# First projection chunk of a decoder trunk: quarters of x and single weight pieces, one token tile at a time

## The chip, the cores and the metric

One core of a Trainium2 chip runs the whole program: one launch, no other core involved. The metric is the device time of one execution in microseconds (us). Shown are the median of three runs and, beside it, one further execution taken by the hardware profiler, from which all rows come.

## The reference, cut to what matters

Two layers of a decoder trunk over 256 tokens of width 1024. Each layer normalizes x, projects it to retention heads, sparse-attention heads and a gated MLP, mixes them, projects back and adds; then it normalizes again and applies a SwiGLU FFN of width 2816.

```python
for l in range(DEPTH):                      # 2
    h = rms_norm(x, attn_norm[l])           # x: (1, 256, 1024)
    proj = h @ w_in[l]                      # 1024 x 3218
    r_q, r_k, r_v, r_g, n_q, n_kv, n_g, gm_z = jnp.split(proj, split_points, axis=-1)
...
    x = x + (mix @ w_out[l]).astype(x.dtype)
    h = rms_norm(x, ffn_norm[l])
    gate, up = jnp.split(h @ w_gate_up[l], 2, axis=-1)
    x = x + ((jax.nn.silu(gate) * up) @ w_down[l]).astype(x.dtype)
```

The change touches only the start of layer 0: the loads of x and of the first weights, the first normalization, and the first chunk of the product with w_in.

## The kernel before, in words

**Products.** All large products are made in three parts. An operand is split into a "hi" part (rounded to fp32r) and a "lo" part (the rest), and hi·hi, lo·hi and hi·lo are added up in a PSUM bank ("acc"). The tokens are two tiles t of 128; the contraction over 1024 is eight steps k of 128. w_in is cut by columns into seven chunks, computed in the order of ORDER; the first, "nk", has 512 columns: keys and values of the sparse attention. So it takes 8 k x 2 tiles x 3 = 48 products of 512 columns.

**Weights.** They stream from DRAM in pieces of one or two k, laid out in the order of use (PIECES; KSPLIT, line 50, gives the k in each piece of a chunk). stream_load (line 484) takes a staging buffer ("wst", at first also four pieces of the tile "PT") and issues the transfer on SP's queue. stream_hi (499) casts it on ScalarE into "whi"; stream_lo (507) subtracts on VectorE into "wlo" and gives the staging buffer back. Six buffers each of whi and wlo.

**x.** It is loaded in four quarters (t, c): tile t and half c of the 1024 columns, that is k 0 to 3 or 4 to 7. norm_first(c) (line 748) waits for both tiles' quarter c, transposes two k of both tiles into one "sm" bank with TensorE, scales by the norm's gain on ScalarE into the hi half of the tile "hcat" (hh) and makes the lo half (hl) on VectorE, 256 columns at a time. The row factor 1/rms (rstd) comes from squares made afterwards and is applied to the products' results.

**Order.** The instructions of each engine stand in the order in which a planner (class Desk) issues them. Every piece of work is a thread that yields operations, waits for events or asks for a buffer. The planner keeps a clock for each engine with costs of its own (_cost_DMA and the like; TensorE's count double until COLD, line 269; the DMA's clock begins at 2000 ns, line 274), always serves the engine that can start first, and there the request of the lowest priority number (rank, line 371). Its costs decide the order, not what is waited for: on the chip each instruction waits for its true inputs, behind what stands before it on its engine.

**The start.** load_start (594) issues the parameters on ScalarE's queue, and on SP's the identity and then the steps of START (line 157): two quarters of x, two weight pieces, two quarters, two pieces; after them the constants. warm_up (579) fills TensorE with products of a zeroed buffer ("w2k") into an sm bank while nothing else is ready, 256 columns wide until the planner's COLD and 128 after, until `started` is set, which project does at its end. In the profile one such filler is two records. setup_bias (659) puts one small product ("rbw") between, for a table of attention biases that goes to DRAM (scr) and comes back as B on SP's queue.

**The first chunk.** project (1442) with apart == "first" goes through k one after another in `both`: hi·hi for both tiles, then lo·hi for both, then hi·lo for both:

```python
            for ev in x_wait[0] + [self.split_hi[i]] if apart else x_wait[1] + [self.ready[i]]:
                yield ev
...
        if apart == "first":
            for k, (i, a) in enumerate(ks):
                yield from both(k, i, a)
```

Of the kernel before, what the change touches and what calls it, by code (L numbers as in the profile page):

```python
# [9 lines left out]
F32 = mybir.dt.float32  # L10
F32R = mybir.dt.float32r
I32 = mybir.dt.int32
AF = mybir.ActivationFunctionType
ALU = mybir.AluOpType
# [32 lines left out]
    "rg": [(_RG, 384)],  # L47
}
ORDER = ["nk", "nq", "gm", "nv", "rq", "rk", "rg"]
KSPLIT = {ORDER[0]: (1, 1, 2, 2, 2), "nv": (3, 3, 2)}  # L50


def _width(name):
# [100 lines left out]


FIRST, SLOT, GRAIN = 16512, 32, 512
START = [(0, 0), (1, 0), "w", "w", (0, 1), (1, 1), "w", "w"]

NR, NREP = 33, 3

# [18 lines left out]
def _free(ap):  # L179
    n = 1  # L180
    for s in ap.shape[1:]:
        n *= s
    return n
# [6 lines left out]
class Engine:  # L190


    def __init__(self, name, eng):
        self.name, self.eng = name, eng

    def __getattr__(self, method):
        fn = getattr(self.eng, method)
# [32 lines left out]
        return 0.833 * _free(a[0]) + (51 if _psum(a[1]) else 93) + 93 * ptr, table  # L230

    def _cost_DMA(self, method, a, k):
        return 4 * _free(a[0]) * a[0].shape[0] / 360.0 + 60, None

    def _cost_SWDMA(self, method, a, k):
        return 1060, None
# [29 lines left out]
class Desk:  # L266
    LAT = {"PE": 170, "DVE": 150, "ACT": 190, "POOL": 200, "DMA": 2000, "SWDMA": 4500}
    TABLE = 1300
    COLD = 5500.0

    def __init__(self, preload):
        self.preload = preload
        self.free = {e: 0.0 for e in self.LAT}
        self.free["DMA"] = 2000.0
        self.pending = {e: [] for e in self.LAT}
        self.table = None
        self.cur = None
        self.live = 0
        self.after = 0
        self.banks = {}  # L280
        self.given = 100
# [116 lines left out]
class Trunk:  # L398
    def __init__(self, ctx, tc, x, wts, cst, oh, relb, par, w1, w2, wsT, out):
        self.ctx, self.tc, self.nc = ctx, tc, tc.nc  # L400
        nc = self.nc
        self.d = dict(x=x, wts=wts, cst=cst, oh=oh, relb=relb, par=par, w1=w1, w2=w2, wsT=wsT, out=out)
        self.PE, self.V = Engine("PE", nc.tensor), Engine("DVE", nc.vector)
        self.A, self.G = Engine("ACT", nc.scalar), Engine("POOL", nc.gpsimd)
        self.SP, self.GQ = Engine("DMA", nc.sync), Engine("SWDMA", nc.gpsimd)

        def preload(table):
            if table == "lnexp":
                nc.scalar.preload_act_table_set("natural_log_exp_and_others")

        self.desk = Desk(preload)
        self.keep = ctx.enter_context(tc.tile_pool(name="keep", bufs=1))
        psum = ctx.enter_context(tc.tile_pool(name="psum", bufs=1, space=bass.MemoryType.PSUM))
        bank = lambda n: psum.tile([128, 512], F32, tag=n, name=n)
        self.acc = Pool([bank(f"acc{i}") for i in range(4)])
        self.sm = Pool([bank(f"sm{i}") for i in range(4)])
        self.norms = 0
        self.kept = 0

        self.pad(FIRST)  # L420
        self.wst = Pool([self.fixed(f"wst{i}", [128, 1024]) for i in range(3)])
        self.whi = Pool([self.fixed(f"whi{i}", [128, 1024], F32R) for i in range(6)])
        self.wlo = Pool([self.fixed(f"wlo{i}", [128, 1024], F32R) for i in range(6)])
        self.w2k = Pool([self.fixed(f"w2k{i}", [128, 512]) for i in range(6)])
        self.w1k = Pool([self.fixed(f"w1k{i}", [128, 256]) for i in range(4)])
        self.x = [self.fixed(f"x{t}", [128, D]) for t in range(2)]
        self.hx = self.fixed("hcat", [128, KD, 2, T], F32R)
        self.hh, self.hl = self.hx[:, :, 0, :], self.hx[:, :, 1, :]
        self.tinies = {}
        n = L * len(PIECES)  # L430
        self.loaded = [Event() for _ in range(n)]
        self.split_hi = [Event() for _ in range(n)]
        self.ready = [Event() for _ in range(n)]
        self.hi, self.lo, self.st = {}, {}, {}
        self.used = 0
        self.started = False
        self.extra = []
# [141 lines left out]
    def warm_up(self):  # L579

        w = yield Need(self.w2k)
        yield self.V.memset(w, 0.0)
        yield self.A.activation(w[:, 511:512], w[:, 510:511], AF.Gelu_apprx_tanh)
        ps = yield Need(self.sm)
        while not self.started:
            n = 256 if self.desk.free["PE"] < Desk.COLD else 128
            yield self.PE.matmul(
                ps[:, :n], w[:, :128], w[:, :n], start=True, stop=True, lat=False,
                prio=lambda: -5 if self.started else 2000,
            )  # L590
        self.desk.give(self.sm, ps)
        self.desk.give(self.w2k, w)

    def load_start(self):
# [150 lines left out]
        self.desk.give(self.w2k, junk)  # L745
        self.desk.fire(ss[c])

    def norm_first(self, c):

        gain = lambda k: self.par[:, P_G1 + k : P_G1 + k + 1]  # L750
        lat = self.desk.LAT
        for t in range(2):
            yield self.ev_x[t][c]
        for ks in ((4 * c, 4 * c + 1), (4 * c + 2, 4 * c + 3)):
            ps = yield Need(self.sm)
            p4 = ps.rearrange("p (k t n) -> p k t n", k=2, t=2)
            yield [
                self.transpose(p4[:, j, t], self.x[t][:, k * 128 : k * 128 + 128])
                for j, k in enumerate(ks)
                for t in range(2)  # L760
            ]
            yield self.ev_par[0]
            split = [Event(), Event()]
            flat = ps.rearrange("p (k n) -> p k n", k=2)

            def low(ps=ps, ks=ks, split=split, flat=flat):
                for j, k in enumerate(ks):
                    yield split[j]
                    yield self.V.scalar_tensor_tensor(
                        self.hl[:, k, :], flat[:, j], gain(k), self.hh[:, k, :].bitcast(F32),  # L770
                        op0=ALU.mult, op1=ALU.subtract, lat=False,
                    )
                    for t in range(2):
                        self.desk.fire(self.hready[t][k], lat["DVE"])
                self.desk.give(self.sm, ps)

            self.desk.fork(low())
            for j, k in enumerate(ks):
                yield self.A.activation(self.hh[:, k, :], flat[:, j], AF.Copy, scale=gain(k), lat=False)
                self.desk.fire(split[j], lat["ACT"])  # L780
                for t in range(2):
                    self.desk.fire(self.hhready[t][k], lat["ACT"])
        for t in range(2):
            junk = yield Need(self.w2k)
            yield self.A.activation(
                junk, self.x[t][:, c * 512 : c * 512 + 512], AF.Square,
                accum_out=self.sums[:, t, c : c + 1], prio=350,
            )
            self.desk.give(self.w2k, junk)
            self.desk.fire(self.ss[t][c])  # L790

    def norm_scale(self):

# [648 lines left out]
    def project(self, pieces, n, apart, then):  # L1442
# [25 lines left out]

        def both(k, i, a):

            x_wait = [[hr[t][k] for t in range(2)] for hr in (self.hhready, self.hready)]
            for ev in x_wait[0] + [self.split_hi[i]] if apart else x_wait[1] + [self.ready[i]]:
                yield ev
            wh, products = self.part(self.hi, i, a), [(self.hh, "hi"), (self.hl, "hi"), (self.hh, "lo")]
            for n_th, (x, half) in enumerate(products):
                if apart and n_th:
                    for ev in x_wait[1] if n_th == 1 else [self.ready[i]]:
                        yield ev
                w = wh if half == "hi" else self.part(self.lo, i, a)
                for t in range(2):  # L1480
                    yield mm(
                        ps[t][:, :n], x[:, k, t * 128 : t * 128 + 128], w,
                        start=k == 0 and n_th == 0, stop=k == KD - 1 and n_th == 2, lat=False,
                    )
            left[i] -= 2
            if left[i] == 0:
                self.done(i)

        if apart == "first":
            for k, (i, a) in enumerate(ks):  # L1490
                yield from both(k, i, a)
        elif apart:
            end = Event(), Event()

            def tile(t):
                for k, (i, a) in enumerate(ks):
                    yield from step(t, k, i, a)
                self.desk.fire(end[t])

            for t in range(2):  # L1500
                self.desk.fork(tile(t))
            for t in range(2):
                yield end[t]
        else:
            for k, (i, a) in enumerate(ks):
                yield from both(k, i, a)
# [165 lines left out]
    def main(self):  # L1672
# [6 lines left out]
        fork(self.stream_hi(), 400)  # L1679
        fork(self.stream_lo(), 400)  # L1680

        for c in range(2):
            fork(self.norm_first(c), 2)
        fork(self.norm_scale(), 4)
        fork(self.setup_bias(), 3)
        for l in range(L):
# [108 lines left out]
```

## Time and profile before

| | us |
|---|---|
| median of 3 runs | 633.23 (633.22, 633.23, 634.04) |
| the profiled execution, its own time | 634.73 |
| its span | 633.0 |
| TensorE (PE) busy in the span | 627.0 |
| VectorE (DVE) busy | 446.7 |
| ScalarE (ACT) busy | 367.1 |

The span runs from the first to the last recorded instruction; 1.7 us of the profiled execution's time lie around it. In the rows further down, PE is TensorE's matmul, PEld its weight load, SPq the issue of a transfer by SyncE. A row of the timeline gives start, length, engine, line, operation, tiles out<-in, and xcount where several were merged; in brackets stands the idle time before it and what ended it. Nearly all instructions have line 203, the helper that makes them, so rows are told apart by their tiles. Lengths of merged matmuls contain the pipeline's tail: the distance from one to the next is read from the chain.

### The profile page before, as it was taken

How to read it: one execution, taken by the hardware profiler on the slowest of the kernel's cores; microseconds unless marked ns; L12 is line 12 of the kernel's file. 1: busy time of each engine (PE TensorE's matmuls, PEld its weight loads, DVE VectorE, ACT ScalarE, POOL GpSimd, SP SyncE). 2: the span in 40 equal slices, each digit the busy share in tenths (PEclk: the TensorE clock that was granted, in tenths of full speed). 3: DMA queues.
4: the chain of work that ended last, by engine and by line, in shares of the span. 5: the costliest groups of instructions: out<-in, count | busy, mean ns of one | idle time of the engine just before them, and what ended most of it. 6: DMA issues, size and time to landing. Idle time of an engine off the chain costs nothing.

```text
span 633.0 us, 9872 instructions
## 1 busy us (share of the span) xinstructions
PE 627.0 (99%) x3638; PEld 536.4 (85%) x3638; DVE 446.7 (71%) x970; ACT 367.1 (58%) x679; POOL 11.3 (2%) x25
## 2 busy tenths in 40 slices
PE   8999999999999999999999999999999999999997
PEld 7889788888889898888888988888889888898886
DVE  3989997685768677664488898866857768676432
ACT  4869843675455565544377795545745555655330
POOL 1120000000000000010000000000000000000000
PEclk9999999999999999999999999999999999999999
DMA  8875144355565656686436522635554655657631
GB/s 300 290 269 159 54 136 157 99 185 182 186 210 168 205 164 210 214 274 218 136 134 209 195 93 56 214 107 159 179 181 152 214 181 178 221 157 236 206 101 66
DMA packets 33599, 111.62 MB, mean 176 GB/s; under 512 B 4291, under 2 KB 5571, under 8 KB 33552
## 3 DMA queue, kind: packets, MB, share of 16 engines
q1 hardware_dynamic: 33232, 110.62, 53.7%
q8 instruction: 28, 0.46, 0.3%
q0 software_dynamic: 176, 0.36, 0.2%
q14 instruction: 19, 0.16, 0.1%
q10 hardware_dynamic: 144, 0.03, 0.0%
HBM read 109.64 MB, written 1.35 MB: 175 GB/s over the span
## 4 chain that ended last, share of the span: by engine, by line
PE 98%; DMA 1%; DVE 0%; SPq 0%; issue 0%
PE acc L203 68%; PE sm L203 30%; DMA x<-in_x_dram 1%; SPq L203 0%; DVE S L203 0%; DVE x L203 0%; DVE amx L203 0%
## 5 line engine op out<-in xcount | busy, mean ns | idle before, releaser
L203 ACT CAST whi<-wst 128x1024 fp32r<-128x1024 f32 (+3 forms) x196 | 201.0, 1029 | 157.9 <-DMA wst<-in_wts_dram 98.4
L203 DVE TENSOR_TENSOR wlo<-wst,whi 128x1024 fp32r<-128x1024 f32 (+3 forms) x196 | 232.0, 1193 | 85.4 <-ACT whi L203 73.1
L203 PE MATMUL acc<-whi,hcat 128*128 128x512 f32 (+2 forms) x512 | 139.4, 379 | 0.0
L203 PEld LDWEIGHTS acc<-whi,hcat 128*128 128x128 f32 x512 | 91.2, 189 | 14.7 <-ACT whi L203 0.6
L203 PE MATMUL acc<-hcat,whi 128*128 128x512 f32 x320 | 99.3, 391 | 0.0
L203 PE MATMUL sm<-hcat,whi 128*128 128x512 f32 x320 | 98.8, 390 | 0.0
L203 PE MATMUL acc<-wlo,hcat 128*128 128x512 f32 (+2 forms) x256 | 79.5, 378 | 0.0
L203 PEld LDWEIGHTS sm<-hcat,whi 128*128 128x128 f32 x320 | 59.9, 188 | 12.6
L203 PEld LDWEIGHTS acc<-hcat,whi 128*128 128x128 f32 x320 | 58.9, 188 | 11.2
L203 PE MATMUL sm<-hcat,wlo 128*128 128x256 f32 x320 | 64.5, 283 | 0.0
L203 PE MATMUL acc<-hcat,wlo 128*128 128x256 f32 x320 | 64.3, 283 | 0.0
L203 PEld LDWEIGHTS acc<-hcat,wlo 128*128 128x128 f32 x320 | 51.2, 191 | 1.6
L203 PEld LDWEIGHTS acc<-wlo,hcat 128*128 128x128 f32 x256 | 46.4, 188 | 6.9
L203 PE MATMUL acc<-whi,ah 128*128 128x512 f32 (+1 forms) x176 | 50.0, 378 | 0.0
L203 PE MATMUL acc<-whi,al 128*128 128x512 f32 (+1 forms) x176 | 50.0, 378 | 0.0
L203 PE MATMUL acc<-wlo,ah 128*128 128x512 f32 (+1 forms) x176 | 49.9, 377 | 0.0
L203 PEld LDWEIGHTS sm<-hcat,wlo 128*128 128x128 f32 x320 | 49.9, 192 | 0.0
L203 DVE TENSOR_TENSOR w2k<-sm,w2k 128x256 f32<-128x256 f32 x40 | 16.9, 423 | 42.6 <-ACT w2k L203 42.6
L203 PEld LDWEIGHTS acc<-whi,al 128*128 128x128 f32 x176 | 31.8, 188 | 5.6
L203 PEld LDWEIGHTS acc<-wlo,ah 128*128 128x128 f32 x176 | 31.8, 188 | 5.5
L203 PEld LDWEIGHTS acc<-whi,ah 128*128 128x128 f32 x176 | 31.7, 188 | 5.4
L203 ACT ACTIVATE hcat<-sm,par 128x128 fp32r<-128x128 f32 (+1 forms) x56 | 17.3, 394 | 11.5 <-PE sm L203 11.1
(213 smaller groups left out, 733.7 us busy)
## 6 DMA issues: line engine op xcount, KB each, us to landing
wst<-in_wts_dram SPq DMA_DIRECT2D x179, 512.0 KB, 4.2
PT<-in_wts_dram SPq DMA_DIRECT2D x7, 512.0 KB, 7.5
wst<-in_wts_dram SPq DMA_DIRECT2D x8, 384.0 KB, 3.1
w<-in_w_dram SPq DMA_DIRECT2D x4, 512.0 KB, 7.7
wst<-in_wts_dram SPq DMA_DIRECT2D x3, 411.0 KB, 4.4
x<-in_x_dram SPq DMA_DIRECT2D x4, 256.0 KB, 5.4
wst<-in_wts_dram SPq DMA_DIRECT2D x4, 256.0 KB, 4.2
B<-scr SPq DMA_DIRECT2D x4, 192.0 KB, 3.8
```

The lines of the kernel that those rows point to most:

```text
L203: return Op(self.name, lambda: fn(*a, **k), dur, table, lat, prio, banks)
```

## The change

- KSPLIT: the first chunk's eight k come in pieces of 1, 1, 1, 1, 2, 2 k in place of 1, 1, 2, 2, 2.
- START: x(0,0), w, x(1,0), w, w, w, x(0,1), x(1,1), w, w. All six pieces of the first chunk now go ahead of the constants; four did of five.
- The planner's transfer costs: 320 in place of 360 bytes per ns while its DMA clock is under 4000 ns, which now begins at 1500.
- The fillers are 128 columns wide throughout, write to an acc bank in place of an sm bank, and end when the first product of the first chunk has been planned.
- norm_first(t) takes the first four k of one tile by itself, 128 columns at a time; norm_second takes the last four k of both tiles, as before, and makes the squares after all of them. Both use `turn`.
- project: for "first" each tile has a thread `high` (hi·hi and lo·hi of each k) and a thread `low` (hi·lo), forked one after the other.

```diff
-KSPLIT = {ORDER[0]: (1, 1, 2, 2, 2), "nv": (3, 3, 2)}
+KSPLIT = {ORDER[0]: (1, 1, 1, 1, 2, 2), "nv": (3, 3, 2)}
...
-START = [(0, 0), (1, 0), "w", "w", (0, 1), (1, 1), "w", "w"]
+START = [(0, 0), "w", (1, 0), "w", "w", "w", (0, 1), (1, 1), "w", "w"]
...
-        return 4 * _free(a[0]) * a[0].shape[0] / 360.0 + 60, None
+        early = self.desk.free["DMA"] < Desk.EARLY
+        return 4 * _free(a[0]) * a[0].shape[0] / (320.0 if early else 360.0) + 60, None
...
+    EARLY = 4000.0
...
-        self.free["DMA"] = 2000.0
+        self.free["DMA"] = 1500.0
...
-        ps = yield Need(self.sm)
+        ps = yield Need(self.acc)
         while not self.started:
-            n = 256 if self.desk.free["PE"] < Desk.COLD else 128
             yield self.PE.matmul(
-                ps[:, :n], w[:, :128], w[:, :n], start=True, stop=True, lat=False,
+                ps[:, :128], w[:, :128], w[:, :128], start=True, stop=True, lat=False,
                 prio=lambda: -5 if self.started else 2000,
             )
...
+    def norm_first(self, t):
+
+        yield self.ev_x[t][0]
+        for k in (0, 2):
+            self.desk.fork(self.turn((t,), (k, k + 1)), 2 + k)
+
+    def norm_second(self):
+
+        for t in range(2):
+            yield self.ev_x[t][1]
+        for k in (4, 6):
+            self.desk.fork(self.turn((0, 1), (k, k + 1)), 2 + k)
+        for t in range(2):
+            yield self.hhready[t][KD - 1]
...
+    def turn(self, tiles, ks):
...
+        ps = yield Need(self.sm)
+        flat = ps[:, : 2 * n * 128].rearrange("p (k n) -> p k n", k=2)
+        yield [
+            self.transpose(flat[:, j, i * 128 : i * 128 + 128], self.x[t][:, k * 128 : k * 128 + 128])
+            for j, k in enumerate(ks)
+            for i, t in enumerate(tiles)
+        ]
...
+        def high(t, begun, end):
+
+            cs = slice(t * 128, t * 128 + 128)
+            for k, (i, a) in enumerate(ks):
+                yield self.split_hi[i]
+                yield self.hhready[t][k]
+                wh = self.part(self.hi, i, a)
+                yield mm(
+                    ps[t][:, :n], self.hh[:, k, cs], wh, start=k == 0, stop=False, lat=False,
+                    prio=1 if k == t == 0 else None,
+                )
+                self.started = True
+                if k == 0:
+                    self.desk.fire(begun)
+                yield self.hready[t][k]
+                yield mm(ps[t][:, :n], self.hl[:, k, cs], wh, start=False, stop=False, lat=False)
+                used(i, 2)
+            self.desk.fire(end)
...
+        def low(t, begun, end, both):
+            yield begun
+            for k, (i, a) in enumerate(ks):
+                if k == KD - 1:
+                    yield end
+                yield self.ready[i]
+                yield self.hhready[t][k]
+                yield mm(
+                    ps[t][:, :n], self.hh[:, k, t * 128 : t * 128 + 128], self.part(self.lo, i, a),
+                    start=False, stop=k == KD - 1, lat=False,
+                )
+                used(i, 1)
+            self.desk.fire(both)
...
         if apart == "first":
-            for k, (i, a) in enumerate(ks):
-                yield from both(k, i, a)
+            left = {i: 3 * n for i, n in left.items()}
+            ends = Event(), Event()
+            for t in range(2):
+                begun, end = Event(), Event()
+                self.desk.fork(high(t, begun, end))
+                self.desk.fork(low(t, begun, end, ends[t]))
+            for t in range(2):
+                yield ends[t]
```

## Rows read from the trace of the kernel before

**Rows 1.** The page: busy time, share of the span and instructions by engine.

```profile
PE 627.0 (99%) x3638; PEld 536.4 (85%) x3638; DVE 446.7 (71%) x970; ACT 367.1 (58%) x679; POOL 11.3 (2%) x25
```

**Rows 2.** Waits of TensorE, whole span: us in total, times, longest.

```profile
PE sm L203 <- DVE w2k L203: 1.4, 1, 1.4
PE sm L203 <- DMA x<-in_x_dram: 1.0, 1, 1.0
PE sm L203 <- DVE amx L203: 0.2, 1, 0.2
```

**Rows 3.** The chain, first 25 us: start, length, what.

```profile
1.63 5.18 DMA x<-in_x_dram
...
6.86 3.46 PE sm L203 x15
...
10.85 0.44 PE sm L203 x4
...
11.76 0.87 PE sm L203 x8
...
14.46 1.67 PE sm L203 x10
16.13 8.39 PE acc L203 x36
24.52 0.22 PE sm L203 x2
```

**Rows 4.** Timeline of TensorE, ScalarE and VectorE, 0 to 16 us.

```profile
1.44 4.21 PE L203 MATMUL sm<-w2k 128*128 128x256 f32 x10 [1.44 <-DVE w2k L203]
7.55 2.77 PE L203 MATMUL sm<-w2k 128*128 128x128 f32 x12
7.51 0.62 ACT L203 CAST whi<-wst 128x512 fp32r<-128x512 f32 x1 [4.86 <-DMA wst<-in_wts_dram]
8.04 0.47 ACT L203 ACTIVATE hcat<-sm,par 128x256 fp32r<-128x256 f32 x1
9.97 0.88 PE L203 MATMUL acc<-whi,hcat 128*128 128x512 f32 x2
10.69 0.61 PE L203 MATMUL sm<-w2k 128*128 128x128 f32 x4
12.24 1.20 ACT L203 ACTIVATE hcat<-sm,par 128x256 fp32r<-128x256 f32 x3 [2.48 <-PE sm L203]
13.11 1.27 DVE L203 SCALAR_TENSOR_TENSOR hcat<-sm,par,hcat 128x256 fp32r<-128x256 f32 x3 [2.83 <-ACT hcat L203]
```

**Rows 5.** SP's issues (start, length), then issue to landing from narrow windows.

```profile
1.16 0.89 SPq L203 DMA_DIRECT2D x<-in_x_dram  x2
2.10 0.91 SPq L203 DMA_DIRECT2D wst<-in_wts_dram  x2
...
4.00 0.43 SPq L203 DMA_DIRECT2D wst<-in_wts_dram  x1
...
x<-in_x_dram SPq DMA_DIRECT2D x1, 256.0 KB, 3.1
wst<-in_wts_dram SPq DMA_DIRECT2D x1, 256.0 KB, 5.4
wst<-in_wts_dram SPq DMA_DIRECT2D x1, 512.0 KB, 6.7
```

**Rows 6.** Timeline of ScalarE in a later norm, halves of 128 columns.

```profile
131.84 1.14 ACT L203 ACTIVATE hcat<-sm,par 128x128 fp32r<-128x128 f32 x4 [1.42 <-PE sm L203]
```

**Rows 7.** A stretch: length, each engine's busy time (instructions), granted clock, DMA share, GB/s.

```profile
6.86:10.30 3.44, 3.44 (x16) 3.44 (x17) 2.11 (x4) 1.98 (x4) 0.46 (x2) 1.00 1.03 392
```

**Rows 8.** Timeline of VectorE after nk, then two stretches as in rows 7.

```profile
24.25 1.22 DVE L203 TENSOR_TENSOR wlo<-PT,whi 128x1024 fp32r<-128x1024 f32 x1
...
20.00:40.00 20.00, 20.00 (x94) 16.52 (x94) 18.33 (x45) 16.16 (x33) 4.26 (x12) 1.00 0.80 268
60.00:80.00 20.00, 19.78 (x160) 15.85 (x158) 18.84 (x97) 17.24 (x63) 0.00 (x0) 1.00 0.21 67
```

More of the change, by code (lines that the diff above doesn't have):

```diff
@@ L190, with __init__ @@
 class Engine:
-    def __init__(self, name, eng):
-        self.name, self.eng = name, eng
+    def __init__(self, name, eng, desk=None):
+        self.name, self.eng, self.desk = name, eng, desk
     def __getattr__(self, method):
@@ L404, in __init__ @@
         self.A, self.G = Engine("ACT", nc.scalar), Engine("POOL", nc.gpsimd)
-        self.SP, self.GQ = Engine("DMA", nc.sync), Engine("SWDMA", nc.gpsimd)
         def preload(table):
@@ L411, in __init__ @@
         self.desk = Desk(preload)
+        self.SP, self.GQ = Engine("DMA", nc.sync, self.desk), Engine("SWDMA", nc.gpsimd)
         self.keep = ctx.enter_context(tc.tile_pool(name="keep", bufs=1))
@@ L583, in warm_up @@
         yield self.A.activation(w[:, 511:512], w[:, 510:511], AF.Gelu_apprx_tanh)
-        ps = yield Need(self.sm)
+        ps = yield Need(self.acc)
         while not self.started:
-            n = 256 if self.desk.free["PE"] < Desk.COLD else 128
             yield self.PE.matmul(
-                ps[:, :n], w[:, :128], w[:, :n], start=True, stop=True, lat=False,
+                ps[:, :128], w[:, :128], w[:, :128], start=True, stop=True, lat=False,
                 prio=lambda: -5 if self.started else 2000,
             )
-        self.desk.give(self.sm, ps)
+        self.desk.give(self.acc, ps)
         self.desk.give(self.w2k, w)
@@ L746, in norm_part @@
         self.desk.fire(ss[c])
-    def norm_first(self, c):
+    def norm_first(self, t):
[10 more added lines that the diff above has]
+        for t in range(2):
+            for c in range(2):
+                junk = yield Need(self.w2k)
+                yield self.A.activation(
+                    junk, self.x[t][:, c * 512 : c * 512 + 512], AF.Square,
+                    accum_out=self.sums[:, t, c : c + 1], prio=350,
+                )
+                self.desk.give(self.w2k, junk)
+                self.desk.fire(self.ss[t][c])
@@ L750, in norm_first @@
+    def turn(self, tiles, ks):
         gain = lambda k: self.par[:, P_G1 + k : P_G1 + k + 1]
         lat = self.desk.LAT
[L752 to L777, printed above, removed]
-            for j, k in enumerate(ks):
[L779 to L790, printed above, removed]
+        n = len(tiles)
+        ts = slice(tiles[0] * 128, tiles[-1] * 128 + 128)
+        ps = yield Need(self.sm)
+        flat = ps[:, : 2 * n * 128].rearrange("p (k n) -> p k n", k=2)
@@ new lines, in turn, with low @@
+        yield [
[3 more added lines that the diff above has]
+        ]
+        yield self.ev_par[0]
+        split = [Event(), Event()]
+        def low():
+            for j, k in enumerate(ks):
+                yield split[j]
+                yield self.V.scalar_tensor_tensor(
+                    self.hl[:, k, ts], flat[:, j], gain(k), self.hh[:, k, ts].bitcast(F32),
+                    op0=ALU.mult, op1=ALU.subtract, lat=False,
+                )
+                for t in tiles:
+                    self.desk.fire(self.hready[t][k], lat["DVE"])
+            self.desk.give(self.sm, ps)
@@ L792, in norm_scale @@
+        self.desk.fork(low())
+        for j, k in enumerate(ks):
+            yield self.A.activation(self.hh[:, k, ts], flat[:, j], AF.Copy, scale=gain(k), lat=False)
+            self.desk.fire(split[j], lat["ACT"])
+            for t in tiles:
+                self.desk.fire(self.hhready[t][k], lat["ACT"])
     def norm_scale(self):
@@ L1469, in both @@
         def both(k, i, a):
-            x_wait = [[hr[t][k] for t in range(2)] for hr in (self.hhready, self.hready)]
-            for ev in x_wait[0] + [self.split_hi[i]] if apart else x_wait[1] + [self.ready[i]]:
+            for ev in [self.hready[t][k] for t in range(2)] + [self.ready[i]]:
                 yield ev
@@ L1475, in both @@
             for n_th, (x, half) in enumerate(products):
-                if apart and n_th:
-                    for ev in x_wait[1] if n_th == 1 else [self.ready[i]]:
-                        yield ev
                 w = wh if half == "hi" else self.part(self.lo, i, a)
@@ L1487, in both, with used @@
                 self.done(i)
-        if apart == "first":
-            for k, (i, a) in enumerate(ks):
-                yield from both(k, i, a)
+        def high(t, begun, end):
[7 more added lines that the diff above has]
+                    prio=1 if k == t == 0 else None,
+                )
+                self.started = True
[5 more added lines that the diff above has]
+            self.desk.fire(end)
+        def used(i, n):
+            left[i] -= n
+            if left[i] == 0:
+                self.done(i)
+        def low(t, begun, end, both):
[8 more added lines that the diff above has]
+                    start=False, stop=k == KD - 1, lat=False,
+                )
+                used(i, 1)
+            self.desk.fire(both)
+        if apart == "first":
+            left = {i: 3 * n for i, n in left.items()}
[4 more added lines that the diff above has]
+                self.desk.fork(low(t, begun, end, ends[t]))
+            for t in range(2):
+                yield ends[t]
         elif apart:
@@ L1680, in main @@
         fork(self.stream_lo(), 400)
-        for c in range(2):
-            fork(self.norm_first(c), 2)
+        for t in range(2):
+            fork(self.norm_first(t), 2)
+        fork(self.norm_second(), 2)
         fork(self.norm_scale(), 4)
```

## The prediction, made before any run of the changed kernel

> **What bounds the kernel now.** I read the page first: TensorE is busy 627.0 of the span's 633.0 us [rows 1]. So a microsecond taken out of TensorE's queue at the head is worth one at the end, unless something later runs dry. Next the waits of TensorE over the whole span: 1.4 us for the first memset, 1.0 for x, 0.2 for a softmax maximum, no more [rows 2]. The first two lie in the head. The head also holds hidden waste, which the chain of the first 25 us shows [rows 3]: x lands, TensorE runs from 6.86 without a break, and the first chunk (nk, 48 products) ends at 24.52 + 0.22 = 24.74. Beside products ("acc") the chain has long stretches of "sm", and the timeline shows what they are [rows 4]: after the first transposes 12 filler records take 2.77 us, 4 more stand at 10.69 and, in the same way, 4 at 14.30 and 2 behind nk. The first product starts at 9.97 though its operands are there by 8.51 (cast begun at 7.51, hcat at 8.04 + 0.47). It stands behind fillers that the planner put in front.
>
> The arrivals set the rest [rows 5]. Issue plus time to landing: x(0,0) 1.16 + 3.1 = 4.26; w0 2.10 + 5.4 = 7.5; the first 512 KB piece 4.00 + 6.7 = 10.7. The chain's wait for x(1,0) ends at 1.63 + 5.18 = 6.81 [rows 3]. Read in the same way, w1 lands at 8.05, x(0,1) at 8.75, x(1,1) at 9.4 and the next 512 KB piece at 11.9. From the second slot on, a 256 KB slot lands some 0.65 us after the one before, a 512 KB slot 1.2 us. Landing follows the slot, so reordering swaps the contents of slots.
>
> **The change part by part.** *Load order.* Slot 1 stays x(0,0) at 4.26. Slot 2 becomes w0, 6.8 in place of 7.5. Then x(1,0) 7.5, w1 8.05, w2 8.75, w3 9.4, x(0,1) 10.05, x(1,1) 10.7, w4 11.9, w5 13.1 (one more 512 KB slot). The last nk weights came after the constants before and now come ahead of them. SP issues one transfer more, at some 0.47 us each (two of x in 0.89), and stays ahead of the data: the last of its first eight is issued at 4.00. The second half of x is 1.3 us later; it is wanted only after 24 products, so I cost that at nothing; without that cover it would cost 1.3.
>
> *Splits and halves on ScalarE and VectorE.* One 1024-wide cast (1.06) becomes two of 512 (0.53 apart): nothing. Four hcat pairs of 256 columns (0.39 apart in the group of three) become eight of 128 (0.28 apart, from a later norm [rows 6]): 2.2 against 1.6, +0.7 us on ScalarE, about the same on VectorE. Both had idle time just there: ScalarE waited 2.48 us for transposes at 12.24, VectorE 2.83 at 13.11 [rows 4]. This covers it.
>
> *First product.* ScalarE's queue is w0's cast, then hcat of tile 0: 6.84 + 0.53 to hcat's start (as from 7.51 to 8.04), + 0.36 (between 0.28 and the 0.47 of the wide form), + 0.05 = 7.8. The operands' bound from below is 7.6, from above 8.5 if w0 lands as late as today.
>
> *Fillers.* They are now always 128 wide and end with the first product. The planner's own costs set only their number: its x(0,0) is due at 4.64, its fillers start at 2.33 and cost 0.43, so six go first, four between the transposes and the first product, one behind it. On the chip twelve records at 0.231 (15 records of transposes and fillers in 3.46 [rows 3]) end at 1.44 + 2.77 = 4.2, then tile 0's four transposes at 4.3 to 5.2, then eight records to 7.05. TensorE then idles to 7.8. Gone are the 4 + 4 records inside nk and the 2 behind it.
>
> *Waits and queue order.* Each tile's hi products wait for their own quarter of x and piece of w; the lo products have a thread of their own, so behind a late w only that tile's next k is queued. By the arrivals w3's cast ends near 11.0 and its lo part near 12.0 (four casts, eight hcat halves from 6.84; as many on VectorE), while 24 products from 7.8 last until past 13. I allow 0.3 us of stalls (between 0 and the 1.0 us that x costs today).
>
> *The sum at full clock.* From the first product: 48 products at 0.233 (36 in 8.39) = 11.2; twelve transposes at 0.109 (8 in 0.87) = 1.3; the bias product 1.67 - 8 x 0.11 = 0.8; one filler 0.2; stalls 0.3: 13.8. nk ends at 7.8 + 13.8 = 21.6 in place of 24.74, a gain of 3.1. The profiled execution took 634.73 (span 633.0 and 1.7 around it): 631.6.
>
> *The clock.* The printed granted clock is 1.00 in every stretch [rows 7], yet a filler record took 0.231 until 10.3 and 0.11 (four in 0.44 [rows 3]) from 10.85 on: durations of the levels 1.2 and 2.4 GHz. Before the rise TensorE had a 1.0 us gap at 5.86 and then ran without a gap from 6.86. In the profiled execution the low level cost nk little beyond 12 x 0.12 = 1.4 us of fillers. The median of the runs is 633.23, 1.5 below the profiled one, about that 1.4. I take it that in those runs the clock rose before 7.5, and that the fillers there cost half; then nk ends at 23.3 there and the gain against the median is 1.7, and 631.5 comes out by both roads. If instead the 1.5 is the profiler's own, the gain is 3.1 and the time 630.1: the low end.
>
> The Trainium skill (TensorE: Matmul & The Clock Gate, Part 1) says the array's default is the half clock, that sustained activity releases it, and that the moment differs between runs of one kernel. This trace agrees on the rise; by it fewer, shorter fillers are a danger, and the sum would be that of rival 1, 633.1, in place of 631.5.
>
> *Downstream.* nk's early end helps only if nq's weights are split in time. The nearest of them is the lo part of nq's second piece, made behind the rstd chain at 24.25 to 25.47 [rows 8]. With nq from 21.6 it is wanted behind two k and four products, 16 x 0.233 later, at 25.3. VectorE's work in front of it starts some 2 us earlier with the rest (its 2.83 us of idling is used), so it is not late; if it did not move, the cost would be 0.2 us.
>
> **The rivals.**
>
> 1. *The clock rises late* (0.22). Products from 7.8 run at half rate until the rise. For it: 0.1 + 0.75 us of gaps ahead of the first product. Against: 1.44 to 7.05 is almost gapless, better than the 1.0 us hole before. At a rise near 11 the loss is (11 - 7.8)/2 = 1.6: nk ends at 23.2 and the time is 633.1.
>
> 2. *VectorE gives it back* (0.12). It is busy 18.33 of 20 us at 20 to 40 and 18.84 at 60 to 80 [rows 8]. If softmax and splits there don't move with TensorE, products wait. Price: all but some 0.3 us of the gain, 632.9. Against: no wait on VectorE over 0.2 us today.
>
> 3. *Slower* (0.11): rival 1 carried on. TensorE's short gaps among the first products, as it waits for each piece, keep the clock low until 15 or later. The loss is (15 - 7.8)/2 = 3.6, nk ends at 25.2 against the 23.3 of the median run: 635.1. It decides from a rise at about 13.8, where the loss of 3.0 exceeds the gain of 1.7 plus 1.3. Against: at half rate each product takes 0.46 and TensorE has no gaps.
>
> 4. *The order does nothing* (0.08): w0 still lands at 7.5, since slot 2 shares the engines with the slots behind. First product 8.5, nk's end 22.3: 632.2.
>
> **How the numbers follow.** Forecast (0.47): 631.5, its own range 630.0 to 632.3. A change within 0.2% (1.3 us) cannot be told from none; faster means below 631.96. Faster: the forecast but for 0.02 of it, all of 0.45, a quarter of rival 2 (0.03), a quarter of rival 1 (0.06) and half of rival 4 (0.04), since their prices are uncertain by that much: 0.58. Slower: rival 3 and a little of rival 2: 0.12. Same: 0.30. The range: low 629.8, under the 630.1; high 633.9, past rivals 1, 2 and 4. It leaves out rival 3 and some 0.08 of tails.
>
> **What would show it.** Right: the cast of w0 at about 6.8; the first acc product near 7.8; no w2k filler behind it; products 0.23 apart from the start; nk's evacuation (the Square of acc) near 21.6; no new TensorE waits after 25. Wrong: early products 0.43 to 0.46 apart (rivals 1, 3); w0's cast at 7.5 (4); a wait of TensorE on VectorE or ScalarE at 25 to 130 (2). A time above 634.5 overturns the argument.

## The result, and the profile after

| | before | after |
|---|---|---|
| median of six runs each | 633.18 us (632.70 to 634.04) | 630.06 us (629.65 to 630.21) |
| the profiled execution | 634.73 | 630.12 |
| its span | 633.0 | 628.3 |
| first product of the first chunk (nk) | 9.97 | 6.62 |
| first product of the second chunk (nq) | 24.5 | 20.6 |
| from there to the span's end | 608.4 | 607.7 |

The ratio is 0.995 (95% interval 0.994 to 0.9961): 3.1 us by the medians, 4.6 between the two profiled executions. The last two rows of the table hold the answer: between these two executions 3.9 us are gained ahead of the second chunk, and what follows is 0.7 us shorter.

The page's busy line of the changed kernel, which answers to [rows 1]:

```profile
PE 623.6 (99%) x3628; PEld 534.0 (85%) x3628; DVE 448.1 (71%) x976; ACT 367.3 (58%) x685; POOL 11.8 (2%) x25
```

All waits of TensorE over its span (us in total, times, longest), against [rows 2]:

```profile
PE acc L203 <- DVE w2k L203: 1.4, 1, 1.4
```

The wait for x is gone, and so is the 0.2 us for a softmax maximum; the view names no wait behind the first filler (short waits among the first products hide in the modelled ends of TensorE's records; the chain runs through one of them). The chain of the first 26 us (start, length, what) answers to [rows 3]:

```profile
2.57 5.07 DMA wst<-in_wts_dram
7.64 0.02 issue
7.66 0.63 ACT whi L203
8.29 0.04 issue
8.33 3.04 PE acc L203 x12
11.37 0.87 PE sm L203 x8
12.24 0.70 PE acc L203 x3
12.94 0.79 PE sm L203 x2
13.73 12.00 PE acc L203 x52
```

Before, the chain passed from x to fillers; now it runs through w1, the second weight piece: landed at 2.57 + 5.07 = 7.64, cast by 8.29, and from 8.33 on the chain shown lies on TensorE alone. All "sm" that is left is the eight late transposes and the bias product. The timeline of TensorE and ScalarE shows the stretch ahead of that, against [rows 4]:

```profile
1.44 2.93 PE L203 MATMUL acc<-w2k 128*128 128x128 f32 x12 [1.44 <-DVE w2k L203]
4.16 1.06 PE L203 MATMUL sm<-cst,x 128*128 128x128 f32 x4
5.01 1.71 PE L203 MATMUL acc<-w2k 128*128 128x128 f32 x8
5.68 0.62 ACT L203 CAST whi<-wst 128x512 fp32r<-128x512 f32 x1 [3.02 <-DMA wst<-in_wts_dram]
6.21 1.13 ACT L203 ACTIVATE hcat<-sm,par 128x128 fp32r<-128x128 f32 x4
6.62 0.50 PE L203 MATMUL acc<-whi,hcat 128*128 128x512 f32 x1
6.96 0.38 PE L203 MATMUL acc<-w2k 128*128 128x128 f32 x2
7.18 0.60 PE L203 MATMUL sm<-cst,x 128*128 128x128 f32 x4
7.53 0.47 PE L203 MATMUL acc<-wlo,hcat 128*128 128x512 f32 x1
```

Issue to landing of the first two transfers behind the identity (issued at 1.16 and 1.63), against [rows 5]:

```profile
x<-in_x_dram SPq DMA_DIRECT2D x1, 256.0 KB, 2.6
wst<-in_wts_dram SPq DMA_DIRECT2D x1, 256.0 KB, 4.0
```

Twelve filler records, four transposes, eight filler records, the first product, one filler, four transposes, a lo product: the order forecast. The cast of w0 starts at 5.68, not at 6.84, and hcat's start 0.53 behind it. From 6.96 on a filler record takes about 0.11 and transposes come 0.11 apart, so the clock had risen to the 2.4 GHz level by the first product; the clock events kept in the trace put the rise at 6.38.

How the second chunk's start is read: the view by stretches, with TensorE's products on hcat alone, counts them from the span's start. Before, then after:

```profile
0.00:24.50 24.50, 12.10 (x48) 1.00 0.83 295
0.00:24.60 24.60, 12.20 (x49) 1.00 0.82 294
```

```profile
0.00:20.50 20.50, 12.02 (x48) 1.00 0.90 326
0.00:20.60 20.60, 12.12 (x49) 1.00 0.89 325
```

The 49th starts between the two. All experiments below are read in this way.

### The profile page after: what moved, and what is told of

Same layout as the page of the kernel before. It is cut to its first block, busy times and chain, and to the rows that moved or that the text cites. A ratio compares the mean times of both kernels' runs of the same rounds, so it can differ in the third digit from the quotient of the medians.

```text
span 628.3 us, 9870 instructions
## 1 busy us (share of the span) xinstructions
PE 623.6 (99%) x3628; PEld 534.0 (85%) x3628; DVE 448.1 (71%) x976; ACT 367.3 (58%) x685; POOL 11.8 (2%) x25
## 4 chain that ended last, share of the span: by engine, by line
PE 98%; DMA 1%; SPq 0%; ACT 0%; DVE 0%; issue 0%
PE acc L203 69%; PE sm L203 29%; DMA wst<-in_wts_dram 1%; SPq L203 0%; ACT whi L203 0%; DVE x L203 0%
## 5 line engine op out<-in xcount | busy, mean ns | idle before, releaser
L203 PE MATMUL acc<-whi,hcat 128*128 128x512 f32 (+2 forms) x512 | 141.8, 380 | 0.1
```

Of the source, the lines that this page charges most:

```text
L203: return Op(self.name, lambda: fn(*a, **k), dur, table, lat, prio, banks)
```

## The experiments

Each was timed in several rounds beside the kernel before, whose medians were 632.94 to 632.99. "49th" is the time of the 49th product, "rest" from there to the span's end, both of the profiled execution. After itself was timed in its six runs alone, not again beside the experiments; before, which was, moved by 0.2 us, so a difference of that size against after says nothing. The halves of hcat by tile and the fillers' bank were not taken back by themselves.

One profile is one draw. By the clock events in the traces the clock rose at 10.33 in the first profile of before, at 9.85 without fillers, and between 5.13 and 7.65 in the twelve other executions; the second transfer's landing scatters too (last section). So the difference between two heads holds some tenths of draw; between the two profiles of before it is 1.5 us.

| kernel | first product | 49th | rest | median us | ratio (95%) |
|---|---|---|---|---|---|
| before, profiled first | 9.97 | 24.5 | 608.4 | 633.18 | |
| before, once more | 8.58 | 23.0 | 608.6 | 633.26 | 1.0009 (0.9999 to 1.002) |
| before + new fillers | 7.63 | 21.6 | 608.1 | 631.68 | 0.9982 (0.9974 to 0.9991) |
| after | 6.62 | 20.6 | 607.7 | 630.06 | 0.995 (0.994 to 0.9961) |
| after, old fillers | 6.67 | 20.9 | 609.6 | 631.65 | 0.9976 (0.9966 to 0.9985) |
| after, no fillers | 7.10 | 22.0 | 607.8 | 632.27 | 0.9989 (0.998 to 0.9998) |
| after, x(1,0) before w0 | 8.02 | 21.2 | 609.6 | 632.97 | 1.0007 (0.9996 to 1.0019) |
| the same, order of all engines kept | 8.31 | 21.9 | 609.2 | 631.82 | 0.9984 (0.9972 to 0.9996) |
| after, tiles together | 7.59 | 20.8 | 607.8 | 630.98 | 0.9967 (0.9954 to 0.998) |
| after, k 2 and 3 in one piece | 7.12 | 20.8 | 608.1 | 630.62 | 0.9963 (0.995 to 0.9976) |
| after, five fillers put back | 6.78 | 21.7 | 607.9 | 631.53 | 0.9983 (0.9974 to 0.9992) |
| after, old planner costs | 7.43 | 20.9 | 607.9 | 630.89 | 0.9968 (0.9956 to 0.9981) |
| after, w0 and w1 first | 6.58 | 20.4 | 607.7 | 629.90 | 0.9951 (0.9938 to 0.9965) |
| the same, first hcat piece ahead | 6.58 | 20.4 | 607.9 | 630.15 | 0.9962 (0.995 to 0.9975) |

**The kernel before, again.** No edit.

> The kernel before, unchanged. Clock theory (the 1.5 us between the profiled execution and the median is the moment at which the clock rises): a second profile shows the time following the 12 filler records after the first transposes: 2.77 us for them goes with some 634.7, 1.4 us with some 633.2, and the unprofiled times spread over 632.7 to 634.7. Profiler theory (the 1.5 us are the profiler's own): the records take 2.77 us again and the profiled execution is again 1.5 us above the others.

The profiled execution took 633.4, among its unprofiled runs (632.57 to 635.41), so the profiler adds nothing that shows. Its timeline of TensorE:

```profile
5.44 0.42 PE L203 MATMUL sm<-cst,x 128*128 128x128 f32 x1
6.31 0.90 PE L203 MATMUL sm<-cst,x 128*128 128x128 f32 x3 [0.45 <-DMA x<-in_x_dram]
7.01 1.81 PE L203 MATMUL sm<-w2k 128*128 128x128 f32 x12
8.58 0.71 PE L203 MATMUL acc<-whi,hcat 128*128 128x512 f32 x2
```

Against [rows 4], x(1,0) landed 0.55 us earlier, and the twelve filler records last 1.81 us in place of 2.77: the clock rose while they ran, at 7.65, where it had risen behind them, at 10.33. Together that is 1.5 us, and the 49th product comes 1.5 us earlier; the span is 1.4 shorter. So the first profile drew late in two things, x(1,0)'s landing and the clock's rise, and the 1.5 us above the median are these two. Against this execution, which lies near the median, after gains 2.4 us ahead of the second chunk (23.0 to 20.6) and 0.9 behind it.

**The fillers.** Three kernels: before with the new fillers alone; after with the old ones; after with none.

```diff
 # before + new fillers
-        ps = yield Need(self.sm)
+        ps = yield Need(self.acc)
         while not self.started:
-            n = 256 if self.desk.free["PE"] < Desk.COLD else 128
             yield self.PE.matmul(
-                ps[:, :n], w[:, :128], w[:, :n], start=True, stop=True, lat=False,
+                ps[:, :128], w[:, :128], w[:, :128], start=True, stop=True, lat=False,
...
-        self.desk.give(self.sm, ps)
+        self.desk.give(self.acc, ps)
...
                         start=k == 0 and n_th == 0, stop=k == KD - 1 and n_th == 2, lat=False,
                     )
+                    self.started = True
```

> Before, with the new fillers alone (128 wide, acc bank, none after the first product). Head theory (the time follows the end of nk, the rest stays 608): the 4 + 4 + 2 records inside and behind nk go, 1.1 us; the first product stays near 10: 632.1. Rival, the re-planned order of the later work makes the gain: no relation to the head, the rest from nk's end on differs from 608.2 by over 1 us.

631.68, 1.3 below before (632.99 beside it): 1.1 was expected. The rest is 608.1, 0.5 below before's second profile; the 49th product moves from 23.0 to 21.6. That the first product would stay near 10 was wrong, it came at 7.63: w0's cast began 0.5 earlier than in before's second profile (6.59 against 7.07) and the clock rose at 5.41, so the twelve records in front of the first product took 1.34 us from start to start, against 1.57 there. How much of this is the fillers' doing and how much the draw, one profile cannot tell. By the medians the fillers alone are worth over a third of the change.

```diff
 # after, old fillers
-        ps = yield Need(self.acc)
+        ps = yield Need(self.sm)
         while not self.started:
+            n = 256 if self.desk.free["PE"] < Desk.COLD else 128
...
-        self.desk.give(self.acc, ps)
+        self.desk.give(self.sm, ps)
...
-                self.started = True
                 if k == 0:
```

> After, with the old fillers alone. Head theory: two transposes of tile 1 now stand ahead of the first product and wait for x(1,0) at 7.0, so it starts at 7.5 to 8 in place of 6.6, and fillers inside nk cost a few tenths: 630.8 to 631.4. Clock theory: 256-wide fillers hold the engine busy as long, the rise stays before 7.5 and nothing is added. Rival (fillers don't matter, the load order is all): 630.1.

631.65, a little above what was expected, and not for the reason given: the first product is as early as in after, and the 49th only 0.3 later. The rest is 1.9 longer. The planner, given other fillers, orders everything behind them anew, and TensorE now waits later on, once between 100 and 140 us and once between 140 and 300:

```profile
PE sm L203 <- DVE w1k L203: 0.6, 1, 0.6
PE acc L203 <- DVE w2k L203: 0.3, 1, 0.3
```

These waits explain half of it. The other half stands as longer busy time of TensorE behind the 49th product, after first (a stretch as in [rows 7]); its cause was not found:

```profile
20.60:628.30 607.70, 604.58 (x3541) 518.30 (x3539) 435.48 (x953) 352.72 (x654) 6.35 (x13) 1.00 0.53 173
20.85:630.50 609.65, 605.54 (x3543) 518.27 (x3541) 435.07 (x952) 352.29 (x654) 6.57 (x13) 1.00 0.53 172
```

The profiled execution (632.32) lies 0.7 above the median, so the median's 1.6 holds less of both.

```diff
 # after, no fillers
-        while not self.started:
+        for _ in range(0):
```

> After without any filler. Clock theory: TensorE is idle until the first transposes near 3.8, the first product near 7.2 and those after it run 0.43 apart until a rise between 10.5 and 14; loss 1.7 to 3.4: 631.8 to 633.5. Head theory without the clock: only the first product is later by 0.3 to 0.6, 630.4 to 630.7.

632.27, in the clock theory's range. Timeline of TensorE:

```profile
6.76 0.69 PE L203 MATMUL sm<-cst,x 128*128 128x128 f32 x2 [1.76 <-DMA x<-in_x_dram]
7.10 0.78 PE L203 MATMUL acc<-whi,hcat 128*128 128x512 f32 x1
...
8.53 0.63 PE L203 MATMUL acc<-wlo,hcat 128*128 128x512 f32 x1
8.96 0.63 PE L203 MATMUL acc<-whi,hcat 128*128 128x512 f32 x1
9.38 0.61 PE L203 MATMUL acc<-wlo,hcat 128*128 128x512 f32 x1
9.81 1.34 PE L203 MATMUL acc<-whi,hcat 128*128 128x512 f32 x5
```

Products start 0.43 apart from 8.53 (8.96, 9.38, 9.81), the 1.2 GHz level, and from then on 0.23 apart: the clock rose at 9.85, sooner than the 10.5 to 14 expected. The first product is 0.5 late, the 37th 0.9 (18.80 against 17.86), the 49th 1.4. The last 0.4 begins at the 38th (19.29), which waits for a lo piece that ends at 19.25, as the chain shows:

```profile
16.87 2.38 DVE wlo L203
```

So of the 0.9 between the first product and the 49th the late clock costs some 0.5, net of what goes with the missing filler and with waits that after has there, and the fillers ahead of the first product earn it. The profiled execution was the fastest of its runs (631.63); the 0.6 up to the median has no trace.

**The load order.**

```diff
-START = [(0, 0), "w", (1, 0), "w", "w", "w", (0, 1), (1, 1), "w", "w"]
+START = [(0, 0), (1, 0), "w", "w", "w", "w", (0, 1), (1, 1), "w", "w"]
```

> After, with x(1,0) ahead of w0 again in the load order, nothing else. Head theory (the first product follows w0's landing): w0 lands at 6.6 to 7.5 in place of 5.6, the first product at 7.5 to 8.5, and since more is at hand by then some 0.5 of stalls go: 1.0 to 1.5 slower, 631.1 to 631.6. Rival (the order of the loads does nothing, the fillers and the clock do it): 630.1.

632.97: the whole gain is gone, twice what was expected. But the 49th product is only 0.6 later. The rest is 1.9 longer, 0.8 of it in longer busy time of TensorE as with the old fillers, with a wait of 1.1 us on VectorE between 100 and 140 us that after has not:

```profile
PE sm L203 <- DVE gml L203: 1.1, 1, 1.1
```

To part the late w0 from the newly planned work, the next kernel swaps only the two transfers on SP's queue; the other engines' order is that of after, instruction by instruction.

```diff
-            yield self.SP.dma_start(st[:, :f], src, lat=False)
+            op = self.SP.dma_start(st[:, :f], src, lat=False)
+            if i == 0:
+                self.held = op.call
+                op.call = lambda: self.nc.sync.dma_start(self.x[1][:, :512], self.d["x"][0, 128:256, :512])
+            yield op
...
+    def early_x(self, op):
+        op.call = self.held
...
-            yield SP.dma_start(self.x[t][:, cs], self.d["x"][0, t * 128 : t * 128 + 128, cs], lat=False)
+            op = SP.dma_start(self.x[t][:, cs], self.d["x"][0, t * 128 : t * 128 + 128, cs], lat=False)
+            if (t, c) == (1, 0):
+                self.early_x(op)
+            yield op
```

> After, with the two transfers of w0 and x(1,0) swapped on SP's queue only: every other engine keeps the order of after, so nothing of the later work is planned anew. Head theory: w0 lands near 7.2 in place of 5.6, the first product near 8.2 in place of 6.6, the first product of the next chunk 0.6 to 1.3 later, and the time by as much: 630.7 to 631.4, with the rest (from the next chunk's first product to the span's end) at 607.7 as in after. Rival (a_xx's 2.9 us are the price of the late w0 itself): 632.5 to 633.

631.82, above the 630.7 to 631.4 of the head theory and well below the rival's 632.5. Its runs spread from 630.73 to 633.65, and the profiled one (632.87) drew late: even x(0,0), whose place was not changed, landed later, so that its transposes waited until 4.72. Timeline of ScalarE and TensorE:

```profile
4.72 1.09 PE L203 MATMUL sm<-cst,x 128*128 128x128 f32 x4 [0.35 <-DMA x<-in_x_dram]
7.37 0.62 ACT L203 CAST whi<-wst 128x512 fp32r<-128x512 f32 x1 [4.72 <-DMA wst<-in_wts_dram]
8.31 0.50 PE L203 MATMUL acc<-whi,hcat 128*128 128x512 f32 x1 [1.34 <-ACT hcat L203]
```

The first product is 1.7 late, the 49th 1.3, and the rest 1.5 longer, 0.8 of it in waits on VectorE after 140 us (Kl 0.6, w2k 0.2), though every engine but SP has the order of after. So w0 in the second slot is worth some 1.3 us at the head in this execution, and the later work gave up another 1.5 without a new plan; that it would stay at 607.7 was wrong. Three of the runs (633.22 to 633.65) show a mean granted clock of 0.997, every other run of the study 0.999 or 1.000: 0.003 of 631 us is some 1.9 us, by our estimate, and would be most of what they lie above the five lowest (630.73 to 631.39). Where the clock was low in them is not known, since they have no trace. How much of the 1.1 us more that x(1,0) before w0 costs by the medians with its own plan is that plan and how much the draws stays open.

**Products tile by tile.** The experiment goes through k for both tiles together, hi·hi, lo·hi, hi·lo, with everything else as after.

```diff
-            for t in range(2):
-                begun, end = Event(), Event()
-                self.desk.fork(high(t, begun, end))
-                self.desk.fork(low(t, begun, end, ends[t]))
...
+            for k, (i, a) in enumerate(ks):
+                yield self.split_hi[i]
+                for t in range(2):
+                    yield self.hhready[t][k]
...
+                    for t in range(2):
+                        yield mm(
+                            ps[t][:, :n], x[:, k, t * 128 : t * 128 + 128], w,
```

> After, with the products of each k made for both tiles together again (loads, pieces, halves and fillers as after). Head theory: the first product waits for tile 1's quarter of x, landed at 7.0, transposed and scaled: 8.0 in place of 6.6, so 0.8 to 1.4 slower, 630.9 to 631.5. Rival (tiles by themselves only reorder the same products): 630.1.

630.98, as expected in size. The first product is 1.0 late, waiting for tile 1, but less is missing by then, and the 49th is 0.2 late in a profiled execution that at 630.4 was the fastest of its runs. The 0.9 by the medians are thus only partly seen in the trace.

**Single pieces.**

```diff
-KSPLIT = {ORDER[0]: (1, 1, 1, 1, 2, 2), "nv": (3, 3, 2)}
+KSPLIT = {ORDER[0]: (1, 1, 2, 2, 2), "nv": (3, 3, 2)}
...
-START = [(0, 0), "w", (1, 0), "w", "w", "w", (0, 1), (1, 1), "w", "w"]
+START = [(0, 0), "w", (1, 0), "w", "w", (0, 1), (1, 1), "w", "w"]
```

> After, with k 2 and 3 in one 512 KB piece again (pieces of 1, 1, 2, 2, 2). Head theory: its cast is done near 10.1 in place of 9.3 for k 2, which is wanted at about 10: 0 to 0.4 slower, 630.1 to 630.5. Rival (single pieces are what lets the products start): 1 us slower or more.

630.62, 0.6 above after, a little more than expected and far from the rival's 1 us. The profiled execution drew a later w0 (cast at 6.18).

**A microsecond at the head.** Five fillers are put back behind products of k 3 to 7, without the planner's knowledge, so that all engines keep the order of after.

```diff
+    def filler(self):
+        ps, w = self.fill_ps, self.fill_w
+        self.nc.tensor.matmul(ps[:, :128], w[:, :128], w[:, :128], start=True, stop=True)
...
                 yield self.hready[t][k]
-                yield mm(ps[t][:, :n], self.hl[:, k, cs], wh, start=False, stop=False, lat=False)
+                op = mm(ps[t][:, :n], self.hl[:, k, cs], wh, start=False, stop=False, lat=False)
+                if t == 0 and k > 2:
+                    op.call = lambda call=op.call: (call(), self.filler())
+                yield op
```

> After, with five fillers (ten records) put back behind products of k 3 to 7 of the first chunk, all engines in the order of after. Head theory (a microsecond at the head is one at the end): 10 x 0.11 = 1.1 slower, 631.2. Rival (the fillers sat in waits that are there anyway): 630.1 to 630.4.

631.53, 1.5 above after; 1.1 was expected. In the profile the 49th product is 1.1 later and the span 1.3 longer (629.6 against 628.3). Up to the bias product, ahead of the fillers, this execution was 0.2 earlier than that of after (12.65 against 12.87), so from there on it lost 1.3. Each of the five fillers stands in the chain with its two records, 0.22 us; the first of them:

```profile
14.40 0.22 PE acc L599 x2
```

Ten records between products, with not one new wait of TensorE, come out whole at the end. The clearest run of the study: here the head's time is the kernel's time.

**The planner's costs.**

```diff
-        return 4 * _free(a[0]) * a[0].shape[0] / (320.0 if early else 360.0) + 60, None
+        return 4 * _free(a[0]) * a[0].shape[0] / (360.0 if early else 360.0) + 60, None
...
-        self.free["DMA"] = 1500.0
+        self.free["DMA"] = 2000.0
```

> After, with the planner's old transfer costs (360 bytes per ns throughout, its DMA clock from 2000). It orders the head a little differently (two of tile 1's transposes go ahead of the first product and wait for x(1,0)). Head theory: the first product 0.3 to 0.8 later, 630.3 to 630.9. Rival (the planner's costs are what orders the later work well): the rest longer than 608.5, 631.5 or more.

630.89, 0.8 above after. One more filler and two of tile 1's transposes go ahead of the first product, which starts at 7.43 although w0's cast began at 5.35; the clock rose at 7.46, later than in after, which has a part in it. The rest is as in after: the costs matter through the order of the head.

**Two attempts to go further.**

```diff
-START = [(0, 0), "w", (1, 0), "w", "w", "w", (0, 1), (1, 1), "w", "w"]
+START = [(0, 0), "w", "w", (1, 0), "w", "w", (0, 1), (1, 1), "w", "w"]
```

> After, with w0 and w1 both ahead of x(1,0). After the first product TensorE waits until 8.33 for w1's cast (landed at 7.64). Head theory: w1 then lands at 7.0 and x(1,0) at 7.6, so some 0.3 of stalls between 6.6 and 8.3 go: 629.6 to 630.0. Rival (tile 1's transposes come too late and take the place of the wait): 630.0 to 630.4.

629.90 (629.78 to 630.27), its 49th product 0.2 earlier than in after. The ranges of the two overlap (after: 629.65 to 630.21), so whether it beats after is not settled.

The last kernel adds to this an hcat piece ahead of the wait for w0, and leaves out the filler behind the first product:

```diff
-        self.free["DMA"] = 1500.0
+        self.free["DMA"] = 1510.0
...
+            op.call = lambda call=op.call: None if self.started else call()
```

> After, with w0 and w1 ahead of x(1,0), the filler behind the first product left out, and the planner's DMA clock from 1510, by which ScalarE makes the first piece of hcat before it waits for w0. Head theory: the first product at 6.2 to 6.4, the next chunk 0.5 to 0.7 earlier than in after: 629.3 to 629.6. Rival (the later work, planned anew, gives it back): 630 to 631.5.

A miss: 630.15. The cast of w0 began at 5.78 there, so the first product could have come by 6.4; it comes at 6.58, behind the eight fillers planned in front of it, and it and the next still run at the low clock level (two in 1.14; the clock rose at 7.51):

```profile
5.01 1.91 PE L203 MATMUL acc<-w2k 128*128 128x128 f32 x8
6.58 1.14 PE L203 MATMUL acc<-whi,hcat 128*128 128x512 f32 x2
5.78 0.62 ACT L203 CAST whi<-wst 128x512 fp32r<-128x512 f32 x1 [0.59 <-DMA wst<-in_wts_dram]
```

## Why the prediction was right, point by point

**The bound.** Right, and shown for one kind of delay: with all engines' order kept, 1.1 us of fillers put into the head moved the end by 1.3 in the profile. With w0 late, in the same order, 1.3 at the head came with 1.5 more behind it, so a microsecond at the head can also cost more than one. Apart from the three kernels whose later waits are named above, the rest from the 49th product on is 607.7 to 608.6.

**Load order and first product.** The mechanism was right, the size off. The step that was off is the term "Slot 2 becomes w0, 6.8 in place of 7.5". It came from one execution, where the second slot took 5.2 us from issue (1.63) to landing. With w0 in it, it took 4.0 in after and 3.7 to 4.5 in the kernels that kept it; with x(1,0) in it, 4.1 to 5.2 in the five that had it there, the first profile of before being the slowest. So the first product came at 6.62, not 7.8, below the bound of 7.6 that the prediction took for its lowest. What stands behind w0 was right to a hundredth: 0.94 us from the start of its cast to the first product, in the forecast (6.84 to 7.78) and in after (5.68 to 6.62), and the same 0.94 with the later cast at 6.18 (k 2 and 3 in one piece) and at 7.37 (swapped transfers).

**Fillers.** Right in number and place: twelve records, eight, one filler behind the first product, none inside nk. The idle time to the first product that was expected did not come, since w0 landed before the fillers ended. The new fillers alone brought 1.3.

**The sum from the first product.** 13.8 was forecast to nk's end, 20.6 - 6.6 = 14.0 came. The wait for w1's cast, which ends at 8.33, takes what the stalls were allowed, and a little more.

**The clock.** The reading of the 1.5 us between profile and median as no artefact of the profiler was right. But only some 1.0 of it, not 1.4, was the fillers' clock (2.77 against 1.81 us); the landing of x(1,0) had its part of 0.55. In after the clock was up by the first product (6.38), so rivals 1 and 3 did not come about. Without fillers rival 1 does: a rise at 9.85, 2.2 us slower than after. The Trainium skill (TensorE: Matmul & The Clock Gate, Part 1) says that the moment of the rise differs between runs of one kernel; two executions of before agree, one with the rise behind the twelve filler records (10.33) and one among them (7.65).

**Downstream.** Right for this plan: no wait of TensorE after 1.44, where before had 0.2. But the rest is 0.7 to 0.9 shorter than in before's two profiles, and the prediction had put nothing there; 0.2 of it is that wait, the cause of the remainder was not found. One of the prediction's signs, the Square of acc near 21.6, came at 21.80, but it does not mark nk's end (20.6): ScalarE stood in two weight casts until then, as its timeline shows:

```profile
19.91 2.00 ACT L203 CAST whi<-wst 128x1024 fp32r<-128x1024 f32 x2
21.80 0.44 ACT L203 ACTIVATE w2k<-acc 128x128 f32<-128x128 f32 x2
```

Rival 2 did not come about here, but other runs show its size: with the old fillers, or x(1,0) first, waits on VectorE of 0.9 and 1.1 us appear, and with the transfers swapped under the same plan 0.8.

**The time.** The sum against the profiled execution gave 631.6; 630.12 came. The 1.5 between are the first product's 1.2 and the 0.7 by which the rest is shorter, less 0.2 in the stalls and 0.2 in where nk's end was read (24.74, while the second chunk's first product starts at 24.55). Against the median the forecast gain was 1.7 and 3.1 came: 2.4 of it ahead of the second chunk and the rest behind it, by before's second profile. That 630.06 is also the 630.1 of the case in which the 1.5 us were the profiler's own is chance, since they were not. Rival 4 (w0 no earlier) was the contrary of what came.

## What to carry to other kernels

In a program whose chain is one engine from its start to its end, a microsecond of that engine's queue at the head was one at the end here, and with a late first weight more than one: look there for work that only keeps the engine busy, and let it end with the first real instruction. Order the first loads by what the first instruction needs, not by kind. A price of a few microseconds at a program's start, where transfers and the clock vary, should be read from more than one execution before it bounds a range.

## What was not expected

- The second 256 KB transfer of the start took between 3.7 and 5.2 us from issue to landing in the fourteen executions profiled here, at the same place in the queue; whether a weight piece, which is one contiguous stretch in DRAM, lands sooner there than a quarter of x (3.7 to 4.5 against 4.1 to 5.2) was not tested by itself.
- A small change at the start is felt 100 us later: the rest varied by up to 1.9 us between plans of the same work, as much as the parts of the change themselves. A new plan is not the only cause: with the planned order kept and two transfers swapped it still grew by 1.5, while with the order kept and fillers put back it grew by 0.2. What decides between the two was not found.
